# The scan of a Mamba-2 layer taken in pairs of chunks, with one stretch of diagonal matmuls in each pair

## The chip, the cores and the metric

The kernel runs on one core of a Trainium2 chip. The metric is the device time of one execution in microseconds; for the kernel before it is the median of three runs, 1520.32 us (1519.99 to 1521.67). One further execution was profiled; every row of a trace below comes from that one.

## The reference

Two layers on a sequence of 1024 tokens of width 1024, with a residual around each and a norm at the end. The first is a spatial-gating layer (a gated MLP that mixes tokens inside chunks of 128), the second a Mamba-2 mixer. The change touches the second alone. Cut to what matters (G = 8 groups, J = 4 heads a group, P = 64 wide, N = 128 states, chunks of 128 tokens):

```python
proj = h @ w_in                                   # z | x, B, C | dt
xbc = silu(causal_depthwise_conv(xbc, conv_w, conv_b))     # 4 taps along the tokens
dA_cs = cumsum(dt * A, axis=2)                    # inside each chunk
decay = exp(where(causal, seg, -inf))             # seg = dA_cs[l] - dA_cs[s]
cb = einsum('bclgn,bcsgn->bclsg', Cm, Bm)
w_ls = cb * decay * dt
y_diag = einsum('bclsgj,bcsgjp->bclgjp', w_ls, x)          # inside a chunk
states = einsum('bclgn,bclgj,bclgjp->bcgjpn', Bm, decay_to_end * dt, x)
prev = scan(carry * chunk_decay + states)         # state before each chunk
y_off = einsum('bclgn,bcgjpn,bclgj->bclgjp', Cm, prev, exp(dA_cs))
y = y_diag + y_off + x * d_skip
gated = rmsnorm(y * silu(z))  per group;  out = gated @ w_out
```

## The kernel before, in words

Large products run in a split form: each float32 operand is written as a high and a low part, and a product is three matmuls (`mm3`, lines 134 to 136). They are also arranged by Strassen-like schemes of seven block products. The Mamba layer first computes some of its projections into DRAM (z, and x, B, C of groups 0, 1, 3 and 5), then runs the scan, `scans()` (lines 1845 to 1962), and then the rest of the output product, `into_end()`.

The scan goes over 64 steps n, group by group, eight chunks c to a group. Small float32 matmuls of a chunk stand between pieces of a large product that fills TensorE: first the projections that are still missing (x, B, C of groups 2, 4, 6, 7, and z of group 7: the generator `projections()`, lines 1392 to 1455), then the first block product of the output (`bo.product(1)`). `project(upto)` runs that filler up to a count of *units*, one unit being six matmuls of 128x512 in the projections and twice three in the output's product; `want(n)` says how many units have run by step n. A projection of 128 channels is eight units and ends in one of two PSUM buffers, `ab`.

The work of a chunk, by method of the class `Scan`:

- `load`: SP loads the decay sums of the chunk, spread over the partitions, into `wl`.
- `decay`: ACT makes the decay matrix of four heads in place, four Relu of 128x128 and an Exp of 128x512 (lines 1594 and 1596).
- `pe_a`: three transposes and the product of B and C into the PSUM tile `tp` (lines 1588 and 1589).
- `tokens`: DVE scales x by dt and masks the product of B and C (lines 1602 and 1604); ACT copies B (line 1606); POOL scales x again for the state (line 1607).
- `weights`: DVE multiplies decay and masked product, 128x512 (line 1612).
- `pe_b`: the *diagonal*, four matmuls with 64 columns each (line 1621), the *off* product of the last state with C (line 1625), and the chunk's *own* contribution to the state (line 1632). Every third and seventh chunk also sums squares for the group's norm with a column of ones (`sum_b`, line 1697). A float32 matmul shows as two passes in the trace.
- `carry` and `update`: POOL decays the state (line 1642), DVE adds the chunk's own part (line 1651, or a copy at line 1649 for chunk 0).
- `out`: DVE scales the off product (line 1663) and adds the skip to the diagonal (line 1666, twice); POOL adds the two (line 1669).
- `gate`: POOL multiplies by silu(z) (line 1673).

The order is written out by hand, each engine runs its instructions in the order of the program, and waits come from the tiles' reads and writes. In PSUM a whole buffer is guarded: a reader on one engine waits for the earlier users of the same buffer on another. Each buffer kind has a fixed count: `sm` (yy, sp, tp) four, `ab` two, `wl` four.

The convolution of a finished projection is a queue of small steps: one on ACT (line 1323), three taps on DVE (line 1317), and per pair of projections one SiLU on ACT (line 1428). `drain()` takes one entry from the queue; `push` joins the first step of a new projection to the queue's last entry, so that a SiLU and the next projection's first step come out together. At the start of a projection everything older than the last one's own steps is drained at once (line 1440), after the next weights have been prepared (line 1453: a cast on ACT, line 111, and a subtraction on POOL, line 112).

Towards the end the operands of the output's product are prepared between the chunks: `bo.ready` scales them by the norm (DVE, line 1750, twice), `bo.prep` splits them (two casts on ACT, two subtractions on DVE, lines 111 and 112). `gate_half` (line 1679) multiplies half of group 7 by silu(z).

Of the kernel before, what the change touches and what calls it, by code (L numbers as in the profile page):

```python
# [11 lines left out]
ALU = mybir.AluOpType  # L12
# [3 lines left out]
P = 128  # L16
# [6 lines left out]
G = 8  # L23
# [6 lines left out]
def kernel(  # L30
# [1528 lines left out]
    class Scan:  # L1559


        def __init__(self, g, eng):
            self.g, self.st, self.eng = g, sts[g], eng
            self.wl, self.tp, self.cw, self.ps, self.state = {}, {}, {}, {}, {}
            if g < G - 1:
                gd.append(dr.tile([P, 2, T], F32, name=f"g_d{g}"))
            else:
                gd.append(self.st["x"])
# [46 lines left out]
        def pe_b(self, c, ends=None):  # L1615

            w, wl = self.cw[c], self.wl.pop(c)
            yy = sm("yy")
            for j in range(4):
                pt, f = j // 2, j % 2  # L1620
                nc.tensor.matmul(out=yy[f * 64:(f + 1) * 64, pt * P:(pt + 1) * P], lhsT=w[:, j * 64:(j + 1) * 64],  # L1621
                                 rhs=wl[:, j, :], start=True, stop=True)
            if c > 0:
                for pt in range(2):
                    nc.tensor.matmul(out=yy[:, 256 + pt * P:384 + pt * P],  # L1625
                                     lhsT=self.state[c - 1][:, pt * P:(pt + 1) * P], rhs=self.x(3, c),
                                     start=True, stop=True)
            sp = None
            if c < 7 or ends is not None:
                sp = sm("sp")  # L1630
            if c < 7:
                nc.tensor.matmul(out=sp[:, 0:256], lhsT=w[:, 512:640], rhs=w[:, 256:512], start=True, stop=True)  # L1632
            if ends is not None:
                ends.sum_b(sp[:, 256:512], 2 if ends.g == G - 1 else 1)
            self.ps[c] = yy, sp
# [10 lines left out]
        def update(self, c):  # L1646
            if c == 0:
                self.state[0] = k1([P, 256], "state")
                V.tensor_copy(out=self.state[0], in_=self.ps[0][1][:, 0:256])
            elif c < 7:  # L1650
                V.tensor_tensor(out=self.state[c], in0=self.ps[c][1][:, 0:256], in1=self.state[c], op=ALU.add)
# [7 lines left out]
        def out(self, c):  # L1659
            yy, t2 = self.ps.pop(c)[0], self.y(c)  # L1660
            if c > 0:
                t1 = k1([P, 2, P], "t1")
                V.tensor_tensor(out=t1, in0=yy[:, 256:512].rearrange("p (m l) -> p m l", m=2),
                                in1=self.st["ze", c // 4][:, 2:4, c % 4 * P:c % 4 * P + P], op=ALU.mult)
            for pt in range(2):
                V.scalar_tensor_tensor(t2[:, pt, :], self.x(pt, c), dsk[:, 2 * self.g + pt:2 * self.g + pt + 1],
                                       yy[:, pt * P:(pt + 1) * P], ALU.mult, ALU.add)
            if c > 0:
                self.eng.tensor_tensor(out=t2, in0=t2, in1=t1, op=ALU.add)
# [23 lines left out]
        def sum_b(self, pr=None, n=1):  # L1693
            pr = sm("pr") if pr is None else pr
            for m in range(n):
                for h in range(2):
                    nc.tensor.matmul(out=pr[h * 64:h * 64 + 1, 0:256], lhsT=ones[:, 0:1],
                                     rhs=self.sq[:, m, h * 256:(h + 1) * 256], start=m == 0, stop=m == n - 1)
            self.sr = self.sq[:, 1, 0:256]
            for h in range(2):  # L1700
                nc.scalar.copy(out=self.sr[h * 64:h * 64 + 1], in_=pr[h * 64:h * 64 + 1, 0:256])
# [143 lines left out]
    def scans():  # L1845
# [41 lines left out]
        drain(len(queue))  # L1887
        project(AHEAD)
        at("pe_a", 1), at("tokens", 1), at("weights", 1)
        at("load", 2)  # L1890
        for n, (g, c) in enumerate(chunks):
            if n == M + 3:
                drain(len(queue))
            elif n == N - 9:
                for k in range(2):
                    bo.get("a", 0, 0, k)
            elif n == N - 7:
                end["scan"] = scan[G - 1]
                bo.get("b", 0, 0, 0)
            p = g if c >= 4 else g - 1  # L1900
            at("pe_b", n, scan[p] if c % 4 == 3 and p >= 0 else None)
            project(want(n + .5))
            at("pe_a", n + 2)
            if n > 0:
                at("weights", n + 1)
            at("update", n)
            at("out", n)
            at("decay", n + 2)
            at("carry", n + 1)
            drain()  # L1910
            at("tokens", n + 2)
            at("gate", n)
            if n >= N - 7:
                k = n - N + 7
                if k % 2:
                    bo.prep(1, k // 2)
                else:
                    bo.ready(0, 0, k // 2)
            at("load", n + 3)
            th = 0 if c >= 4 else 1  # L1920
            if p >= 0:
                sc = scan[p]
                if p == G - 1:
                    if c == 5:
# [6 lines left out]
            if c % 4 == 0 and n >= 8:  # L1931
                scan[g - 1].sum_c(1 - th)
# [19 lines left out]
        bo.prep(1, 3)  # L1952
# [63 lines left out]
```

## Time and profile before

| | |
|---|---|
| median of three runs | 1520.32 us (1519.99 to 1521.67) |
| the profiled execution | 1518.62 us, its span 1516.8 us |
| clock of TensorE in it | 0.995 of full |
| the scan's 64 chunks | 1020.6 to 1359.4 us of the span |
| busy in the span | PE 97%, DVE 69%, ACT 52%, POOL 27% |

Starts are counted from the span's first instruction. PE is TensorE, DVE is VectorE, ACT is ScalarE, POOL is GpSimd, SP issues the DMAs. A row of the timeline shows the start, the length up to the end of the last of its instructions, the engine, the line, the operation, what it writes and reads, its form and how many instructions it joins; in brackets stands the idle time before it and what ended it. Matmuls are pipelined, so their lengths overlap, and the distance from start to start is what one costs. For a matmul 128*64 means 128 rows and 64 columns of the array.

### The profile page before, as it was taken

What the parts mean: (1) busy time and instruction counts of PE and PEld (TensorE: products, weight loads), DVE (VectorE), ACT (ScalarE), POOL (GpSimd) and SP (SyncE); (2) the same over time, 40 slices, a digit from 0 to 9 for tenths busy, and PEclk for the clock granted to TensorE, in tenths of its full rate; (3) what the DMA queues carried; (4) which work ended last, traced back from release to release, by engine and by line L of the source; (5) the groups of instructions that cost most, each with busy time, mean ns of one, the idle gap of its engine ahead of it and who ended that gap; (6) DMA issues with size and microseconds to landing.
All of it is one profiled execution on the core that took longest, in us unless ns stands there. A gap on an engine that the chain in (4) does not pass through costs nothing. (4 is left out here: it accounts for less than half of the span.)

```text
span 1516.8 us, 21309 instructions
## 1 busy us (share of the span) xinstructions
PE 1475.7 (97%) x7834; PEld 1219.7 (80%) x7834; DVE 1051.7 (69%) x1713; ACT 782.8 (52%) x1257; POOL 402.5 (27%) x451
## 2 busy tenths in 40 slices
PE   6899999999999999999999999999999999999997
PEld 6899988888888888877778888877777777777875
DVE  6966567676666655678656467867677776688876
ACT  6533332232323445556565556666676666756463
POOL 1111010000000023202131222217677666643121
PEclk9999999999999999999999999999999999999999
DMA  5554323323322999947277978677656564579973
GB/s 183 140 167 139 111 90 103 116 103 103 116 77 86 356 251 244 258 139 160 98 179 155 201 153 167 144 245 202 188 162 173 160 189 137 168 252 278 258 151 111
DMA packets 174952, 254.45 MB, mean 168 GB/s; under 512 B 16400, under 2 KB 103168, under 8 KB 171648
## 3 DMA queue, kind: packets, MB, share of 16 engines
q1 hardware_dynamic: 124768, 168.93, 36.1%
q0 software_dynamic: 42448, 70.27, 23.1%
q10 hardware_dynamic: 7632, 13.90, 2.5%
q8 instruction: 62, 1.02, 0.3%
q14 instruction: 42, 0.34, 0.1%
HBM read 186.14 MB, written 51.18 MB: 156 GB/s over the span
## 5 line engine op out<-in xcount | busy, mean ns | idle before, releaser
L134 PE MATMUL acc<-hh,wh 128*128 128x512 f32 x868 | 340.3, 392 | 2.5 <-ACT u L296 2.0
L136 PE MATMUL acc<-hh,wl 128*128 128x512 f32 x868 | 338.6, 390 | 2.0 <-DVE wl L112 1.8
L135 PE MATMUL acc<-hl,wh 128*128 128x512 f32 x868 | 337.9, 389 | 0.0
L112 DVE TENSOR_TENSOR wl<-wr,wh 128x1024 fp32r<-128x1024 f32 (+1 forms) x96 | 114.3, 1192 | 119.0 <-ACT wh L111 118.8
L136 PEld LDWEIGHTS acc<-hh,wl 128*128 128x128 f32 x868 | 162.9, 188 | 37.9 <-DVE wl L112 3.7
L134 PEld LDWEIGHTS acc<-hh,wh 128*128 128x128 f32 x868 | 163.0, 188 | 37.3 <-ACT u L296 3.6
L135 PEld LDWEIGHTS acc<-hl,wh 128*128 128x128 f32 x868 | 163.1, 188 | 33.2
L296 ACT COPY u<-acc 128x512 f32<-128x512 f32 x115 | 66.7, 582 | 198.5 <-PE acc L136 198.3
L111 ACT CAST wh<-wr 128x1024 fp32r<-128x1024 f32 (+1 forms) x112 | 115.2, 1029 | 95.7 <-PE acc L135 56.7
L136 PE MATMUL acc<-wh,hl 128*128 128x256 f32 x448 | 129.3, 289 | 4.0 <-DVE hl L407 3.5
L134 PE MATMUL acc<-wh,hh 128*128 128x256 f32 x448 | 129.6, 289 | 3.2 <-DVE wh L418 1.6
L135 PE MATMUL acc<-wl,hh 128*128 128x256 f32 x448 | 128.7, 287 | 1.3 <-DVE wl L421 1.3
L134 PE MATMUL ab<-hh,wh 128*128 128x512 f32 x288 | 128.2, 445 | 1.5 <-DVE x L1317 1.1
L136 PE MATMUL ab<-hh,wl 128*128 128x512 f32 x288 | 113.4, 394 | 0.0
L135 PE MATMUL ab<-hl,wh 128*128 128x512 f32 x288 | 112.4, 390 | 0.0
L136 PEld LDWEIGHTS acc<-wh,hl 128*128 128x128 f32 x448 | 87.8, 196 | 5.2 <-DVE hl L407 4.2
L134 PEld LDWEIGHTS acc<-wh,hh 128*128 128x128 f32 x448 | 87.8, 196 | 4.2 <-ACT hh L400 1.9
L135 PEld LDWEIGHTS acc<-wl,hh 128*128 128x128 f32 x448 | 87.8, 196 | 1.7 <-DVE wl L421 1.5
L1594 ACT ACTIVATE wl<-wl,tk 128x128 f32<-128x128 f32 x256 | 81.6, 391 | 1.5 <-DMA wl<-cs_d 1.3
L649 POOL DMA_DIRECT2D y_d<-y x8 | 4.4, 548 | 290.7 <-DVE y L646 290.7
L135 PE MATMUL bo<-wl,xh 128*128 128x512 f32 x192 | 75.9, 395 | 3.9 <-DVE wl L742 2.1
L112 DVE TENSOR_TENSOR wl<-t,wh 128x1024 fp32r<-128x1024 f32 (+1 forms) x38 | 45.4, 1196 | 47.7 <-ACT wh L111 47.6
(316 smaller groups left out, 3251.1 us busy)
## 6 DMA issues: line engine op xcount, KB each, us to landing
wr<-in_a_w_in_dram SPq DMA_DIRECT2D x48, 512.0 KB, 3.7
wl<-cs_d SPq DMA_DIRECT2D x64, 256.0 KB, 3.3
wr<-in_b_w_in_dram SPq DMA_DIRECT2D x30, 512.0 KB, 7.7
wb<-in_a_w_out_dram SPq DMA_DIRECT2D x10, 1024.0 KB, 10.9
wb<-in_b_w_out_dram SPq DMA_DIRECT2D x10, 1024.0 KB, 11.1
wr<-in_b_w_in_dram SPq DMA_DIRECT2D x36, 256.0 KB, 7.1
v<-v_d SPq DMA_DIRECT2D x8, 1024.0 KB, 4.9
y_d<-y POOLq DMA_DIRECT2D x8, 1024.0 KB, 5.7
```

The source lines that it names most:

```text
L111: nc.scalar.copy(out=hi, in_=src)
L112: return (eng or nc.vector).tensor_tensor(out=lo, in0=src, in1=hi.bitcast(F32), op=ALU.subtract)
L134: nc.tensor.matmul(out=o, lhsT=l[0], rhs=r[0], start=start, stop=False, **kw)
L135: nc.tensor.matmul(out=o, lhsT=l[0], rhs=r[1], start=False, stop=False, **kw)
L136: nc.tensor.matmul(out=o, lhsT=l[1], rhs=r[0], start=False, stop=stop, **kw)
L296: nc.scalar.copy(out=self.u[n][:, i], in_=a)
L649: store = lambda: nc.gpsimd.dma_start(out=y_d[-1], in_=y)
L1594: nc.scalar.activation(wl[:, j, :], wl[:, j, :], AF.Relu, scale=-1.0, bias=tokc(2, c, self.g)[:, j:j + 1])
```

## The change

The chunks are taken in pairs, the even one n and the odd one n+1:

- `pe_b` becomes three methods. `diagonal(n)` does the diagonals of both chunks, into one `yy` buffer; `own` and `off` write one buffer `os` and are called for each chunk on its own. In the even step comes the diagonal, then own and off of n; in the odd step own and off of n+1, followed at once by `pe_a`.
- `out` becomes `skip` (the skip and the diagonal, for both chunks in the even step) and `out` (the off product and the sum).
- `sum_b` goes behind the diagonal, a chunk later than before, with 64 columns of ones in place of one, into a buffer of its own; `sum_c`, which stores its result, follows in the same step.
- The convolution's `drain` comes first on DVE in the even step, and after `out` and `gate` in the odd one.
- `decay` runs three chunks ahead instead of two, and ahead of the filler and of `out`; `weights` two ahead instead of one; `load` goes out in pairs, four and five ahead.
- Carrying and updating the state come ahead of `out`.
- The output's operands (`ready`, `prep`) and `gate_half` of group 7's first half come a chunk sooner, the fourth `prep` inside the loop.
- Before the loop, `pe_a`, `tokens` and `weights` of chunk 1 come ahead of the filler.

```diff
-        def pe_b(self, c, ends=None):
+        def diagonal(self, c):
...
+            yy = sm("yy")
+            for e in range(2):
+                w, wl = self.cw[c + e], self.wl.pop(c + e)
+                self.yy[c + e] = yy[:, e * 256:(e + 1) * 256]
+                for j in range(4):
+                    pt, f = j // 2, j % 2
+                    nc.tensor.matmul(out=self.yy[c + e][f * 64:(f + 1) * 64, pt * P:(pt + 1) * P],
+                                     lhsT=w[:, j * 64:(j + 1) * 64], rhs=wl[:, j, :], start=True, stop=True)
+        def own(self, c):
+            w = self.cw[c]
+            if c < 7:
+                self.os[c] = sm("os")
+                nc.tensor.matmul(out=self.os[c][:, 0:256], lhsT=w[:, 512:640], rhs=w[:, 256:512],
+                                 start=True, stop=True)
+        def off(self, c):
+            if c == 7:
+                self.os[c] = sm("os")
             if c > 0:
                 for pt in range(2):
-                    nc.tensor.matmul(out=yy[:, 256 + pt * P:384 + pt * P],
+                    nc.tensor.matmul(out=self.os[c][:, 256 + pt * P:384 + pt * P],
...
+        def skip(self, c):
+            yy, t2 = self.yy.pop(c), self.y(c)
             for pt in range(2):
                 V.scalar_tensor_tensor(t2[:, pt, :], self.x(pt, c), dsk[:, 2 * self.g + pt:2 * self.g + pt + 1],
                                        yy[:, pt * P:(pt + 1) * P], ALU.mult, ALU.add)
+        def out(self, c):
+            os, t2 = self.os.pop(c), self.y(c)
             if c > 0:
+                t1 = k1([P, 2, P], "t1")
+                V.tensor_tensor(out=t1, in0=os[:, 256:512].rearrange("p (m l) -> p m l", m=2),
+                                in1=self.st["ze", c // 4][:, 2:4, c % 4 * P:c % 4 * P + P], op=ALU.mult)
                 self.eng.tensor_tensor(out=t2, in0=t2, in1=t1, op=ALU.add)
...
-                    nc.tensor.matmul(out=pr[h * 64:h * 64 + 1, 0:256], lhsT=ones[:, 0:1],
+                    nc.tensor.matmul(out=pr[h * 64:h * 64 + 64, 0:256], lhsT=ones[:, 0:64],
...
+        at("pe_a", 1), at("tokens", 1), at("weights", 1)
         project(AHEAD)
-        at("pe_a", 1), at("tokens", 1), at("weights", 1)
-        at("load", 2)
+        at("load", 2), at("load", 3)
+        at("decay", 2)
         for n, (g, c) in enumerate(chunks):
...
-            at("pe_b", n, scan[p] if c % 4 == 3 and p >= 0 else None)
-            project(want(n + .5))
-            at("pe_a", n + 2)
-            if n > 0:
-                at("weights", n + 1)
-            at("update", n)
+            if c % 2 == 0:
+                at("diagonal", n)
+                if c % 4 == 0 and g > 0:
+                    scan[g - 1].sum_b()
+                elif n == N - 2:
+                    scan[g].sum_b(n=2)
+                at("own", n), at("off", n)
+                at("load", n + 4), at("load", n + 5)
+                drain()
+                at("skip", n), at("update", n)
+                at("carry", n + 1)
+                at("skip", n + 1)
+                project(want(n + .5))
+                at("pe_a", n + 2)
+                if c % 4 == 0 and g > 0:
+                    scan[g - 1].sum_c(1 if c else 0)
+            else:
+                at("own", n), at("off", n)
+                at("pe_a", n + 2)
+                at("update", n)
+                at("carry", n + 1)
+            at("tokens", n + 2)
+            at("weights", n + 2)
+            at("decay", n + 3)
+            if c % 2:
+                project(want(n + .5))
             at("out", n)
-            at("decay", n + 2)
-            at("carry", n + 1)
-            drain()
-            at("tokens", n + 2)
             at("gate", n)
-            if n >= N - 7:
-                k = n - N + 7
+            if c % 2:
+                drain()
+            if n >= N - 8:
+                k = n - N + 8
                 if k % 2:
                     bo.prep(1, k // 2)
                 else:
                     bo.ready(0, 0, k // 2)
-            at("load", n + 3)
...
-                    if c == 5:
+                    if c == 4:
                         sc.gate_half(th), sc.squares(th)
...
-            if c % 4 == 0 and n >= 8:
-                scan[g - 1].sum_c(1 - th)
...
-        bo.prep(1, 3)
         sc.gate_half(1), sc.squares(1)
```

More of the change, by code (lines that the diff above doesn't have):

```diff
@@ L1563, in __init__ @@
             self.g, self.st, self.eng = g, sts[g], eng
-            self.wl, self.tp, self.cw, self.ps, self.state = {}, {}, {}, {}, {}
+            self.wl, self.tp, self.cw, self.yy, self.os, self.state = {}, {}, {}, {}, {}, {}
             if g < G - 1:
@@ L1613, in weights @@
                             op=ALU.mult)
-        def pe_b(self, c, ends=None):
-            w, wl = self.cw[c], self.wl.pop(c)
+        def diagonal(self, c):
             yy = sm("yy")
[L1619 to L1622, printed above, removed]
+            for e in range(2):
[14 more added lines that the diff above has]
+                self.os[c] = sm("os")
             if c > 0:
                 for pt in range(2):
-                    nc.tensor.matmul(out=yy[:, 256 + pt * P:384 + pt * P],
+                    nc.tensor.matmul(out=self.os[c][:, 256 + pt * P:384 + pt * P],
                                      lhsT=self.state[c - 1][:, pt * P:(pt + 1) * P], rhs=self.x(3, c),
                                      start=True, stop=True)
[L1628 to L1635, printed above, removed]
         def carry(self, c):
@@ L1648, in update @@
                 self.state[0] = k1([P, 256], "state")
-                V.tensor_copy(out=self.state[0], in_=self.ps[0][1][:, 0:256])
+                V.tensor_copy(out=self.state[0], in_=self.os[0][:, 0:256])
             elif c < 7:
-                V.tensor_tensor(out=self.state[c], in0=self.ps[c][1][:, 0:256], in1=self.state[c], op=ALU.add)
+                V.tensor_tensor(out=self.state[c], in0=self.os[c][:, 0:256], in1=self.state[c], op=ALU.add)
         def y(self, c):
@@ L1657, in y @@
             return self.cw[c][:, 768:1024].rearrange("p (m l) -> p m l", m=2)
[L1659 to L1664, printed above, removed]
+        def skip(self, c):
+            yy, t2 = self.yy.pop(c), self.y(c)
             for pt in range(2):
@@ L1896, in scans @@
                     bo.get("a", 0, 0, k)
+            elif n == N - 8:
+                bo.get("b", 0, 0, 0)
             elif n == N - 7:
                 end["scan"] = scan[G - 1]
-                bo.get("b", 0, 0, 0)
             p = g if c >= 4 else g - 1
-            at("pe_b", n, scan[p] if c % 4 == 3 and p >= 0 else None)
-            project(want(n + .5))
-            at("pe_a", n + 2)
-            if n > 0:
-                at("weights", n + 1)
-            at("update", n)
+            if c % 2 == 0:
[24 more added lines that the diff above has]
+                project(want(n + .5))
             at("out", n)
-            at("decay", n + 2)
-            at("carry", n + 1)
-            drain()
-            at("tokens", n + 2)
             at("gate", n)
-            if n >= N - 7:
-                k = n - N + 7
+            if c % 2:
+                drain()
+            if n >= N - 8:
+                k = n - N + 8
                 if k % 2:
```

## The prediction, made before the changed kernel was run

> **What bounds the kernel now.** I read first the page's span, then the windows of the scan, then the waits of TensorE inside it, then the timelines.
>
> ```profile
> span 1516.8 us, 21309 instructions
> ```
>
> ```profile
> 1020.60:1309.60 289.00, 286.81 (x1745) 219.11 (x1744) 210.00 (x437) 195.03 (x406) 200.52 (x222) 1.00 0.61 170
> 1309.60:1359.40 49.80, 48.87 (x301) 36.13 (x301) 38.33 (x81) 35.53 (x71) 23.43 (x29) 1.00 0.76 254
> ```
>
> The columns of the windows are the stretch, its length, and the busy time of PE, weight loads, DVE, ACT and POOL. The first is chunks 0 to 53 of the scan, the second chunks 54 to 63. TensorE is busy throughout at full clock, DVE 210.00 of 289.00 us in the first and 38.33 of 49.80 us in the second. TensorE sets the time; it hardly waits:
>
> ```profile
> PE ab L134 <- DVE x L1317: 1.1, 2, 0.7
> PE bo L135 <- DVE wl L112: 0.7, 1, 0.7
> PE sp L1697 <- POOL gsq L1691: 0.5, 1, 0.5
> ```
>
> That is 2.3 us in 338.8. So an edit gains what it takes off TensorE's own stream, as long as the other engines still deliver ahead of it.
>
> **What the change takes off TensorE.** One chunk (number 25), by start times:
>
> ```profile
> 1154.19 0.39 PE L136 MATMUL ab<-hh,wl 128*128 128x512 f32 x1
> 1154.51 0.66 PE L1621 MATMUL yy<-wl,cw 128*64 128x128 f32 x8
> 1155.09 0.71 PE L1625 MATMUL yy<-xbc,state 128*128 128x128 f32 x4
> 1155.64 0.60 PE L1632 MATMUL sp<-cw 128*128 128x256 f32 x2
> 1155.89 0.58 PE L134 MATMUL ab<-hh,wh 128*128 128x512 f32 x1
> 1156.31 0.39 PE L135 MATMUL ab<-hl,wh 128*128 128x512 f32 x1
> 1156.54 0.40 PE L136 MATMUL ab<-hh,wl 128*128 128x512 f32 x1
> ...
> 1157.46 0.49 PE L1588 MATMUL tp<-ident,xbc 128*128 128x128 f32 x3
> 1157.79 0.39 PE L1589 MATMUL tp<-xbc 128*128 128x128 f32 x2
> ```
>
> A projection matmul takes 0.23 us (1156.31 to 1156.54), so a unit of six takes 1.4; a 128-column pass takes 0.11 (three from 1157.46 to 1157.79), so pe_a takes 0.55. Around the diagonal, the only 128*64 work, time is lost three times: 0.32 into it instead of 0.23; its eight passes, two column halves at once, take 0.58 instead of 4 x 0.11; the four passes after it 0.55 instead of 0.44. That is 0.09 + 0.14 + 0.11 = 0.34 us a stretch. With 32 stretches instead of 64 the gain is 32 x 0.34 = 10.9 us. Into and out of pe_a nothing is lost, so stretches of other float32 work may move freely.
>
> [...]
>
> ```profile
> 1165.61 0.60 PE L1632 MATMUL sp<-cw 128*128 128x256 f32 x2
> 1166.13 0.60 PE L1697 MATMUL sp<-gsq,ones 128*1 128x256 f32 x4
> 1166.66 0.50 PE L134 MATMUL ab<-hh,wh 128*128 128x512 f32 x1
> 1167.00 0.39 PE L135 MATMUL ab<-hl,wh 128*128 128x512 f32 x1
> ```
>
> The norm's sum (128*1, another mode) makes L1632 to L135 1.39 us instead of 0.67 (1155.64 to 1156.31): 0.72. Behind the diagonal with 64 columns it is in the diagonal's mode: two pairs of 256-column passes at (0.67 - 0.23) / 2 = 0.22, so 0.44; if they didn't pair, 0.88 (a loss of 0.16 each). The 128*1 passes start in pairs, four in 0.53, so I take 0.44: 15 sums in the scan x 0.28 = 4.2 us. If all 2.3 us of waits goes too, the gain is 10.9 + 4.2 + 2.3 = 17.4 us.
>
> **What the new order makes late.** A pair on TensorE, from the first diagonal: eight diagonal pitches 0.9; exit and first load 0.2, own 0.44, off 0.44: 2.0; a unit, 3.4; pe_a(n+2), 3.95; a unit, 5.35; own and off of the odd chunk, 6.2; pe_a(n+3), 6.8; two units, 9.6. DVE's steps are these:
>
> ```profile
> 1166.43 0.41 DVE L1602 TENSOR_TENSOR cw<-tp,tk 128x256 f32<-128x256 f32 x1
> 1166.76 0.27 DVE L1604 TENSOR_TENSOR cw<-tp,mask 128x128 f32<-128x128 f32 x1
> 1167.12 0.95 DVE L1612 TENSOR_TENSOR wl<-wl,cw 128x512 f32<-128x512 f32 x1
> 1168.10 0.42 DVE L1651 TENSOR_TENSOR state<-sp,state 128x256 f32<-128x256 f32 x1
> 1168.45 0.41 DVE L1663 TENSOR_TENSOR t<-yy,ze 128x256 f32<-128x256 f32 x1
> 1168.78 0.60 DVE L1666 SCALAR_TENSOR_TENSOR cw<-xbc,dsk,yy 128x128 f32<-128x128 f32 x2
> 1169.29 1.27 DVE L1317 SCALAR_TENSOR_TENSOR x<-ab,par,x 128x1021 f32<-128x1021 f32 x1
> ```
>
> In the odd chunk tokens start at 7.1 and take 0.7, weights end at 8.75, the off product's scaling (L1663) at 9.1 and the tap, now last, at 10.3. The next diagonal, at 9.7, needs only the weights: an ordinary pair holds, with 0.9 us to spare. The first tap, the skips and the update of the even chunk end near 3.3, ahead of pe_a(n+2). So the 32 pairs cost nothing in themselves; four places do.
>
> *The buffer of ab.* A product's first unit writes the buffer that the third tap of the product two before it read. A product (128 channels) is 8 units; by chunk c 16 + 112c/50 of them have run, rounded down, half a chunk counting too. Its steps join the queue after its eighth unit, and each drain takes one. Counted so from the code, units 33, 65 and 105, each the first of a product, are the second unit of the odd chunks 7, 21 and 39, and the third tap that they wait for is the drain of the same chunk. TensorE is there at 6.8 + 1.4 = 8.2; the tap ends at 10.3. Before, a tap stood ahead of tokens, and no such wait shows at these chunks. Three times 2.0 is 6.0 us (with the tap early, 0).
>
> *A tap that waits for ACT.* Where a group's SiLU is forced out by a new product, ACT does this:
>
> ```profile
> 1080.72 1.05 ACT L111 CAST wh<-wr 128x1024 fp32r<-128x1024 f32 x1
> 1081.79 1.28 ACT L1428 ACT_TABLE_LOAD   x1
> 1083.08 1.91 ACT L1428 ACTIVATE bc<-bc 128x2048 f32<-128x2048 f32 x1
> 1085.02 1.21 ACT L1323 ACTIVATE x<-ab,par 128x1024 f32<-128x1024 f32 x1
> 1086.13 1.27 ACT L1594 ACTIVATE wl<-wl,tk 128x128 f32<-128x128 f32 x4
> 1087.41 1.28 ACT L1596 ACT_TABLE_LOAD   x1
> 1088.70 0.63 ACT L1596 ACTIVATE wl<-wl 128x512 f32<-128x512 f32 x1
> ```
>
> ```profile
> 1086.26 1.28 DVE L1317 SCALAR_TENSOR_TENSOR x<-ab,par,x 128x1023 f32<-128x1023 f32 x1 [4.21 <-ACT x L1323]
> ```
>
> This is chunk 11: the tap waits 4.21 us, and none of the waits above is for the weights behind it. After the change the forced part stands behind decay(14), which ends at 9.9 (tokens, a copy, 1.9 of decay): cast, table, SiLU and convolution's first step end at 15.2, or 5.6 in the next pair. Queued behind that tap on DVE are a second tap, the skips and update(12), done at 8.9; off(13) wants that state at 7.6: 1.3 us. Tokens(14) follow at 9.4, and ACT's decay(15) behind them, with its table load 3.2 us, ends at 13.4, the weights at 14.4; TensorE is there at 12.8: 1.6. Chunk 11 costs 2.9. At chunk 25 the next pair has a unit less ahead of off, which is there at 5.8 against 8.9, and 1.6 again: 4.7. Chunk 46, worked likewise, 2.4. At 4, 18 and 32 the part falls ahead of a decay with room. Bounds: 0, as now, and 10.0; I take 9, nearest the end that the written order gives.
>
> *The last chunks.* Here DVE has little room, since the output's operands join it:
>
> ```profile
> 1346.13 1.23 DVE L112 TENSOR_TENSOR xl<-ya,xh 128x1024 fp32r<-128x1024 f32 x1 [1.74 <-ACT xh L111]
> ...
> 1350.72 1.92 DVE L1750 SCALAR_TENSOR_TENSOR ya<-ya,par,rb 128x512 f32<-128x512 f32 x2
> ```
>
> A chunk sooner they end the odd chunk, so their casts stand on ACT behind decay(n+3) instead of ahead of the next one's, and their splits (1.23 each) ahead of the next pair's skips. After chunk 57 DVE splits from 2.9 to 5.2 in pair 58; then skips, update, tokens, weights, scaling, the scale of 1.9, update, tokens and weights again end at 11.6, where TensorE, with three units, is ready at 8.5. In pair 60, behind z's SiLU, the splits begin at 4.7; off waits 1.8, and with gate_half (1024 columns, so about a split's 1.23) the weights are 2.8 late. Together 7.7. The lower bound is the 0.7 of wait that this part has now; I take 7. Earlier operands (prep at 59 instead of 60) remove that 0.7, already in the 2.3.
>
> *The rest.* Two taps flushed ahead of chunk 53's update: 0 to 2, taken 1. The loads go out on SP two at a time, behind the wait for the diagonal, 1.0 us into the pair; behind them queue sum_c, the stores and the prefetches, which nobody awaits inside the pair.
>
> ```profile
> wl<-cs_d SPq DMA_DIRECT2D x64, 256.0 KB, 3.3
> ```
>
> They land near 5, and the first decay that reads them stands behind tokens(n+3), at 8: nothing lost, and 1 us a pair if landing took twice as long. In the prologue pe_a(1) only moves ahead of seven units.
>
> **Sum.** 6 + 9 + 7 + 1 = 23 against 17.4: 5.6 us longer. The profiled execution took 1518.62 us (span 1516.8); the median of the runs shown, 1520.32, lies 1.7 above it. 1518.6 + 5.6 + 1.7 = 1525.9; with the roundings, all upward by a tenth or two, 1525.
>
> **Rivals.** *The stream alone decides* (faster): at chunks 11, 25, 46 and in the last ten DVE, 73% busy in the first window, catches up within the pair, and only the waits for ab stand: 1520.3 - 17.4 + 6 = 1508.9, or 1502.9 without them. The point is whether the even chunk's update ends before the odd chunk's off product, about 6 us into the pair. For it speak TensorE's 286.81 of 289.00 us, and that chunk 11 costs nothing that the waits show now; against it, that taps and splits queue in order ahead of update and weights. Chance 0.17. *Half*: waiting taps cost nothing, the rest stands: 1525 - 9 = 1516; with half the tail too, 1512.5. Chance 0.2. *More contention* (slower still): the product of weights spreads from 678 to 1983 ns.
>
> ```profile
> L1612 DVE TENSOR_TENSOR wl<-wl,cw x63: 678/951/1983, 1021.8 to 1353.7; 128x512 f32<-128x512 f32 x63
> ```
>
> At the longest it ends 1.0 us later than worked above, 0.1 past the 0.9 to spare; with POOL behind too, 0.3 us in 25 pairs gives 1533. Chance 0.1. *The modes don't pair*: sums at 0.88 and no gain from them: 6.6 us more, 1532; 0.03. The forecast keeps 0.5, with its own range from 1519 to 1533.
>
> **How the numbers follow.** A measurement tells about 0.2% from no change, here 3 us: 1517.3 to 1523.3. Faster: 0.17, and two thirds of the 0.2, makes 0.3. Same: the rest of it and the lower end of the forecast, 0.21. Slower: 0.49. The range 1508 to 1533 leaves out a tenth at either end.
>
> **What would show it.** Right: TensorE's shortest chunk pair shorter by 0.3, diagonals of 16 in a row; waits of ab's matmul for a tap near 2 us, three times; of the off product for the state; of the diagonal for weights; waits in the scan of 15 us or more. Wrong: waits under 8 us there, or the last ten chunks shorter than 48 us; then the time is under 1517.

## The result, and the profile after

The changed kernel is slower: 1533.39 us in the median of four runs (1530.39 to 1534.85), against 1520.28 us before (1519.99 to 1521.67, four runs). The ratio is 1.0087, with a 95% interval of 1.0075 to 1.0099: 13.1 us longer. I had forecast 1525 with a range from 1508 to 1533, so the direction came out and the size did not: about 5 us were forecast and 13 measured.

The profiled execution after took 1533.07 us. Its span, and the windows that answer the two shown of before (columns: the stretch, its length, busy PE, weight loads, DVE, ACT, POOL, then the granted clock):

```profile
span 1531.4 us, 21280 instructions
```

```profile
1020.60:1316.60 296.00, 279.42 (x1745) 226.06 (x1744) 213.07 (x432) 192.61 (x407) 196.72 (x220) 0.99 0.59 166
1316.60:1373.00 56.40, 48.71 (x303) 38.40 (x303) 42.62 (x88) 37.92 (x72) 27.03 (x31) 0.97 0.71 225
```

The span is 14.6 us longer. Chunks 0 to 53 take 296.0 us in place of 289.0, the last ten 56.4 in place of 49.8, and 1.0 us is lost behind the scan. TensorE's busy time in the first stretch fell from 286.81 to 279.42 us: the gain is there. But TensorE now stands still for 16.6 us of that stretch instead of 2.2, and the clock is no longer 1.00 in either. The waits of TensorE (what waits and for whom; us in total, times, the longest):

```profile
PE yy L1623 <- DVE wl L1612: 9.6, 8, 2.5
PE os L1640 <- DVE state L1658: 6.0, 4, 3.0
PE ab L134 <- DVE bc L1317: 5.4, 3, 2.1
...
PE os L1631 <- issue: 2.4, 2, 1.6
...
PE ab L134 <- DVE x L1317: 0.9, 1, 0.9
```

These are 24.3 us, where the same view of before has 2.9 in all (its three largest rows are the prediction's 2.3). The diagonal (line 1623) waits for the weights, the off product (line 1640) for the state, a projection's first matmul for the tap that still reads its buffer. The stream itself looks as forecast; this is where a pair begins, chunk 16, on TensorE:

```profile
1105.36 1.22 PE L1623 MATMUL yy<-wl,cw 128*64 128x128 f32 x16
1106.40 0.60 PE L1706 MATMUL pr<-gsq,ones 128*64 128x256 f32 x4
```

Sixteen diagonal passes stand in a row, 1.04 us from first to the next line, where two stretches of eight took 0.58 each, with two entries and two exits around them. A pair of chunks with four units and no wait takes 9.60 us from diagonal to diagonal, in place of 9.97.

And these are the places where TensorE stands still in the scan (the bracket is its idle time and what ended it):

```profile
1060.25 0.50 PE L134 MATMUL ab<-hh,wh 128*128 128x512 f32 x1 [1.64 <-DVE bc L1317]
...
1091.37 0.49 PE L1640 MATMUL os<-xbc,state 128*128 128x128 f32 x2 [1.25 <-DVE state L1658]
...
1096.61 0.44 PE L1623 MATMUL yy<-wl,cw 128*64 128x128 f32 x4 [0.60 <-DVE wl L1612]
...
1119.55 0.50 PE L134 MATMUL ab<-hh,wh 128*128 128x512 f32 x1 [0.93 <-DVE x L1317]
...
1139.11 0.50 PE L134 MATMUL ab<-hh,wh 128*128 128x512 f32 x1 [1.71 <-DVE bc L1317]
...
1169.81 0.58 PE L1640 MATMUL os<-xbc,state 128*128 128x128 f32 x1 [3.03 <-DVE state L1658]
...
1213.61 0.38 PE L1640 MATMUL os<-bc,state 128*128 128x128 f32 x1 [0.73 <-DVE state L1658]
...
1219.86 0.33 PE L1623 MATMUL yy<-wl,cw 128*64 128x128 f32 x2 [1.59 <-DVE wl L1612]
...
1240.74 0.50 PE L134 MATMUL ab<-hh,wh 128*128 128x512 f32 x1 [2.05 <-DVE bc L1317]
...
1292.04 0.45 PE L1631 MATMUL os<-cw 128*128 128x256 f32 x1 [1.58 <-issue]
...
1296.63 0.44 PE L1623 MATMUL yy<-wl,cw 128*64 128x128 f32 x4 [0.73 <-DVE wl L1612]
...
1306.99 0.44 PE L1623 MATMUL yy<-wl,cw 128*64 128x128 f32 x4 [0.54 <-DVE wl L1612]
...
1318.18 0.44 PE L1623 MATMUL yy<-wl,cw 128*64 128x128 f32 x4 [0.95 <-DVE wl L1612]
...
1348.16 0.66 PE L1623 MATMUL yy<-wl,cw 128*64 128x128 f32 x8 [2.53 <-DVE wl L1612]
...
1354.44 0.67 PE L1631 MATMUL os<-cw 128*128 128x256 f32 x2 [0.79 <-issue]
...
1356.06 0.71 PE L1640 MATMUL os<-bc,state 128*128 128x128 f32 x4 [0.95 <-DVE state L1658]
...
1363.13 0.43 PE L1623 MATMUL yy<-wl,cw 128*64 128x128 f32 x3 [2.46 <-DVE wl L1612]
```

The rows at 1060.25, 1139.11 and 1240.74 are the buffer of `ab`, in chunks 7, 21 and 39. Those at 1091.37 and 1096.61, at 1169.81, and at 1292.04 are the taps that wait for ACT, after chunks 11, 25 and 46 (at 1292.04 the trace names no releaser; DVE's tap waited 3.57 us for ACT just before). The rows at 1213.61 and 1219.86 are of the same kind, after chunk 32, where I had said there was room. The row at 1119.55, in chunk 18, is a fourth wait for the buffer of `ab`: the product's first unit stands there in the even chunk, and two taps come in a row on DVE ahead of it, the last of chunk 17 and the first of chunk 18. From 1296.63 to 1318.18 three pairs in a row wait for weights. The last four are the tail. The wait at chunk 18, and then the largest of the body (1169.81), on DVE (the bracket is DVE's idle time):

```profile
1116.91 2.58 DVE L1317 SCALAR_TENSOR_TENSOR x<-ab,par,x 128x1022 f32<-128x1022 f32 x2
...
1166.31 2.60 DVE L1317 SCALAR_TENSOR_TENSOR x<-ab,par,x 128x1023 f32<-128x1023 f32 x2 [6.02 <-ACT x L1323]
...
1169.34 0.42 DVE L1658 TENSOR_TENSOR state<-os,state 128x256 f32<-128x256 f32 x1
```

At 1166.31 DVE has stood still for 6.02 us in front of a tap, with the skips and the state's update queued behind it, and the off product starts when the state is there. At the tail's first large wait it is the scale of the output's operands that stands in the way:

```profile
1344.59 1.87 DVE L1759 SCALAR_TENSOR_TENSOR ya<-ya,par,rb 128x512 f32<-128x512 f32 x2
1346.38 0.41 DVE L1658 TENSOR_TENSOR state<-os,state 128x256 f32<-128x256 f32 x1
...
1347.41 0.69 DVE L1612 TENSOR_TENSOR wl<-wl,cw 128x512 f32<-128x512 f32 x1
```

The weights at 1347.41 are what the diagonal at 1348.16 waits for.

One thing was not in my sum at all. Behind three of the waits TensorE runs on at 0.54 to 0.57 of its clock; the fourth window is behind the wait of 2.53 us (the clock is the third number from the end):

```profile
1169.90:1173.50 3.60, 3.60 (x14) 3.33 (x15) 3.10 (x9) 2.61 (x6) 2.33 (x4) 0.57 0.07 25
1240.80:1244.80 4.00, 4.00 (x22) 3.03 (x24) 1.88 (x4) 3.97 (x4) 3.92 (x4) 0.57 0.00 0
1364.20:1367.80 3.60, 3.60 (x15) 2.52 (x12) 3.34 (x7) 0.94 (x3) 1.11 (x1) 0.54 0.81 299
...
1348.20:1351.80 3.60, 3.60 (x27) 2.86 (x28) 0.24 (x1) 3.55 (x7) 1.06 (x2) 1.00 0.49 182
```

In 3.6 us at 0.57 some 1.5 us of work are lost, an estimate (3.6 x 0.43); the three together are 1.5 + 1.7 + 1.7 = 4.9 us.

### The profile page after: what moved, and what is told of

Its sections match the earlier page's. It is cut to its first block, busy times and chain, and to the rows that moved or that the text cites. A ratio compares the mean times of both kernels' runs of the same rounds, so it can differ in the third digit from the quotient of the medians.

```text
span 1531.4 us, 21280 instructions
## 1 busy us (share of the span) xinstructions
PE 1466.5 (96%) x7834; PEld 1227.5 (80%) x7834; DVE 1057.5 (69%) x1713; ACT 781.1 (51%) x1257; POOL 400.9 (26%) x451
## 5 line engine op out<-in xcount | busy, mean ns | idle before, releaser
L134 PE MATMUL ab<-hh,wh 128*128 128x512 f32 x288 | 122.4, 425 | 8.0 <-DVE bc L1317 5.4
```

The lines of the kernel that those rows point to most:

```text
L134: nc.tensor.matmul(out=o, lhsT=l[0], rhs=r[0], start=start, stop=False, **kw)
```

## The experiments

My theory after the result: the gain on TensorE's stream is real, the body's loss comes from where the convolution's steps stand on DVE, the tail's loss from the output's operands coming a chunk sooner, and the halved clock from the waits themselves. The rivals: DVE is short of time however it is ordered; the tail's loss is the pairing; the halved clock has another cause; TensorE's stream does not decide. Times are medians, ratios are against the kernel before, measured beside each. Traces are of one execution each. Pair lengths are the distances between the first diagonal passes of the pairs, and "the tail" is the time from chunk 54's diagonal to the output's eighth unit: 48.6 us before and 55.2 after.

### The sums alone, in the old buffer

In the kernel before, the sum takes 64 columns of ones and goes from the end of `pe_b` to between the diagonal and the off product:

```diff
-                    nc.tensor.matmul(out=pr[h * 64:h * 64 + 1, 0:256], lhsT=ones[:, 0:1],
+                    nc.tensor.matmul(out=pr[h * 64:h * 64 + 64, 0:256], lhsT=ones[:, 0:64],
...
+            if ends is not None:
+                ends.sum_b(sp[:, 256:512], 2 if ends.g == G - 1 else 1)
```

> The kernel before, with one part of the change alone: the sums take 64 columns of ones and stand right behind the diagonal stretch, so no switch of tile shape lies between them. If a switch costs what the rows of before gave (0.28 us for each of 15 sums), the time falls by 4.2 us, from 1520.3 to 1516.1, and the sums' two passes start 0.21 us apart. If TensorE's stream does not decide at these places, the time stays at 1520.3 within 1 us.

1527.33 us, ratio 1.0054 (1.0034 to 1.0073): neither. The pairs with a sum and no new wait are shorter by 0.28 us, 9.97 in place of 10.25, which is the term. But there is a new row among the waits of TensorE:

```profile
PE sp L1634 <- ACT gsq L1701: 7.1, 7, 2.7
```

The chunk's own product writes the other half of the sum's buffer, and now waits until ACT has copied the sum out of it. So the buffer was to be separated.

### The sums alone, in a buffer of their own

The same edit, with `sum_b` called so that it takes a buffer itself:

```diff
-                ends.sum_b(sp[:, 256:512], 2 if ends.g == G - 1 else 1)
+                ends.sum_b(n=2 if ends.g == G - 1 else 1)
```

> The kernel before, with the sums as after the change: 64 columns of ones, right behind the diagonal, and now in a buffer of their own, so that the chunk's own product no longer waits for ScalarE to copy the sum out. If a switch of tile shape costs 0.28 us for each of 15 sums, 1516.1. If the gain is swallowed by another wait, 1520.3 or more.

1517.27 us against 1518.85, ratio 0.9987 (0.9978 to 0.9997). The waits for the copy are gone, and the gain is 1.6 us of 4.2. At one place most of the rest goes: the pair of chunk 50 takes 14.1 us in place of 11.3, with this row in TensorE's timeline:

```profile
1292.89 0.44 PE L1697 MATMUL pr<-gsq,ones 128*64 128x256 f32 x2 [1.84 <-POOL gsq L1691]
```

The sum now stands ahead of the off product, and POOL has not yet added the squares. The clock in the 3.6 us behind this wait was 0.61.

### The same, with chunk 51's sum last again

```diff
+            at51 = ends is not None and (ends.g, c) == (5, 3)
-            if ends is not None:
+            if ends is not None and not at51:
                 ends.sum_b(n=2 if ends.g == G - 1 else 1)
...
+            if at51:
+                ends.sum_b()
```

The second call stands behind the chunk's own product.

> The kernel before, with the sums as after the change in a buffer of their own, but in chunk 51, where the sum behind the diagonal waited 1.8 us for GpSimd's addition and the pair took 14.1 us against 11.3, the sum stands last again. If that one place took the rest of the gain, it falls from 1517.3 by about 2.8 to 1514.5. If the gain of a switch was only 1.6 us in all, it stays at 1517.

1516.48 us against 1519.30, ratio 0.9985 (0.9976 to 0.9994). It is faster than both kernels. The pair of chunk 50 fell from 14.1 to 11.6 us, but the time lies between the two that were expected, and its interval overlaps that of the run above. The medians differ by 2.8 us, the profiled scan (first diagonal to the output's eighth unit) is 334.3 us against 337.6, 3.2 shorter. So two thirds to three quarters of the term of 4.2 are there, and it is the part of the change that pays alone.

### The diagonals apart again

```diff
-            for e in range(2):
-                w, wl = self.cw[c + e], self.wl.pop(c + e)
+            w, wl = self.cw[c], self.wl.pop(c)
...
-                at("own", n), at("off", n)
+                at("diagonal", n), at("own", n), at("off", n)
                 at("pe_a", n + 2)
-                at("update", n)
+                at("skip", n), at("update", n)
```

The last lines are those of the odd step.

> The kernel after, with one part undone: each chunk's diagonal in its own step again, with a buffer of its own, all else in pairs. If the fewer switches gave the 10.9 us that the rows of before say, and a diagonal that comes 6 us later no longer waits for its weights (9.6 us of waits, of which I take 5 to 8 away), the time is 1533.4 + 10.9 less 5 to 8, 1536 to 1539. If the fewer switches gave nothing, because VectorE decides, it is 1525 to 1533.

1544.83 us, ratio 1.0165 (1.0148 to 1.0182): 11.4 us more than with pairs, where I expected 3 to 6. The pairs without a wait are longer by 0.33 to 0.37 us (9.15 to 9.52, 10.97 to 11.30), so the gain of 0.34 a stretch is confirmed. The waits for weights are no longer among the longest, and the tail falls to 51.2. In their place this stands among the waits of TensorE:

```profile
PE tp L1588 <- DMA xbc<-xbc_d: 9.0, 5, 3.1
```

The transposes wait for the prefetched x, B and C. That the odd chunk's skip, a step later here, holds the buffer longer and so delays the prefetch fits, but is only argued.

### The output's operands later again

```diff
-            if n >= N - 8:
-                k = n - N + 8
+            if n >= N - 7:
+                k = n - N + 7
...
-                    if c == 4:
+                    if c == 5:
                         sc.gate_half(th), sc.squares(th)
```

(The load of the first weights and the fourth `prep` also go back to their places of before.)

> The kernel after, with one part undone: the output's operands (scale, casts, splits, the last gate) a chunk later, as in the kernel before. If this part is what lengthens the stretch from chunk 54 to the output's eighth unit from 48.6 to 55.2 us, that stretch falls back by 5 to 6.6 us and the time to 1527 to 1528. If it is the pairing, which asks for the weights of two chunks at once, the stretch stays at 55 and the time at 1533.

1537.02 us, ratio 1.0120 (1.0100 to 1.0140). Neither: the tail rose to 59.6 us instead of falling. The earlier operands are worth 4.4 us to the paired order, and my theory of the tail falls.

### The last ten chunks apart

```diff
-                at("diagonal", n)
+                at("diagonal", n, 2 if n < N - 10 else 1)
...
+                if n >= N - 10:
+                    at("diagonal", n, 1)
```

The last two lines stand first in the odd step.

> The kernel after, with the diagonals of the last ten chunks apart again, each in its own step. If it is the pairing that lengthens the tail, since it asks for the odd chunk's weights 5 us sooner, the stretch from chunk 54 to the output's eighth unit falls from 55.2 to about 51, as with all diagonals apart, and the time to 1529. If VectorE's work in those chunks is too much however it is ordered, the stretch stays above 54 and the time at 1532 to 1535.

1529.87 us, ratio 1.0074 (1.0059 to 1.0089), as expected of the pairing. From chunk 54 on, to the same point, in the window that answers the one of 56.40 us:

```profile
1317.50:1370.00 52.50, 48.62 (x303) 37.18 (x303) 41.13 (x88) 37.81 (x72) 27.01 (x30) 1.00 0.73 242
```

52.5 us in place of 56.4, at full clock, though each pair has its second switch again. (The difference rests on the profiles: the intervals of the two ratios overlap.) In this order the scale ahead of the odd chunk's weights hurts only if the next diagonal wants those weights at once. That the pairing alone lengthens the tail does not follow: the next two runs keep the diagonals of the tail in pairs, and their tails are 50.7 and 51.7 us.

### Both steps in the middle of the pair

```diff
-                drain()
                 at("skip", n), at("update", n)
                 at("carry", n + 1)
                 at("skip", n + 1)
+                drain(), drain()
...
-            if c % 2:
-                drain()
```

> The kernel after, with both convolution steps of a pair behind the even chunk's update and second skip, in place of one first and one last. If the order on VectorE is the cause, the waits of the projection's first matmul for a tap (6.3 us) and of the off product for the state (6.0 us) go, with the slow clock behind two of them (3 us), and a part, some 3 to 5 us, comes back as waits of the diagonal for weights, since the tokens now stand behind a tap that waits for ScalarE: 1521 to 1524. If VectorE is short of time altogether, the waits only change their place: 1531 to 1535.

1542.42 us, ratio 1.0154 (1.0126 to 1.0181): worse than either theory. The waits of TensorE:

```profile
PE yy L1623 <- DVE wl L1612: 12.7, 11, 2.5
...
PE ab L134 <- DVE x L1317: 9.2, 4, 3.6
...
PE ab L134 <- DVE bc L1317: 4.0, 2, 2.3
```

The waits for the state are gone, but those for the taps grew from 6.3 to 13.2 us, and those for weights from 9.6 to 12.7. ACT holds the taps up less than before: up to chunk 54 DVE waits for ACT's first step 9.2 us in all, where it waited 34.2 in the change. Both taps now stand behind the skips and the update, so they end later; at chunk 18, on DVE and then on TensorE:

```profile
1120.89 2.59 DVE L1317 SCALAR_TENSOR_TENSOR x<-ab,par,x 128x1022 f32<-128x1022 f32 x2
```

```profile
1123.53 0.79 PE L134 MATMUL ab<-hh,wh 128*128 128x512 f32 x1 [3.61 <-DVE x L1317]
```

### The steps five microseconds apart

```diff
-            if c % 2:
+            if c % 2 == 0:
                 drain()
```

> The kernel after, with the pair's second convolution step at the end of the even chunk's work instead of the odd one's, so that the steps stand some 5 us apart. If the steps' places are the cause of the body's loss, the waits for a tap's buffer (5.4 us) go, most of those for the state (6.0 us) too, and with them the halved clock behind two of them (3 us): 1520 to 1524. If a step ahead of the odd chunk's update only makes that update and the weights late, the waits for weights grow by as much: 1531 to 1536.

1528.51 us, ratio 1.0065 (1.0047 to 1.0082), between the two. The three waits for `ab` at chunks 7, 21 and 39 are gone but for 0.2 us at chunk 7, and at chunk 54 the kernel is 1.9 us ahead of the change (294.1 against 296.0). But now others come, at chunks 32 and 46 among them. DVE and then TensorE in the timeline at chunk 32:

```profile
1199.48 1.27 DVE L1317 SCALAR_TENSOR_TENSOR x<-ab,par,x 128x1021 f32<-128x1021 f32 x1
```

```profile
1200.81 0.50 PE L134 MATMUL ab<-hh,wh 128*128 128x512 f32 x1 [3.79 <-DVE x L1317]
```

Here the third tap is the step at the end of the even chunk, and the new product begins in that chunk's second half, ahead of it.

The edit reaches the tail too, where the queue still hands out z's SiLU. In the change the last of it comes out at the end of chunk 59, ahead of the casts of the output's operands; here no step is taken there, and it comes out at the start of chunk 60, behind them. ACT in the change, and then here:

```profile
1350.80 1.03 ACT L1418 ACTIVATE z<-ab 128x1024 f32<-128x1024 f32 x1
1351.72 1.04 ACT L111 CAST xh<-ya 128x1024 fp32r<-128x1024 f32 x1
```

```profile
1348.85 1.03 ACT L111 CAST xh<-ya 128x1024 fp32r<-128x1024 f32 x1
...
1352.78 1.02 ACT L1418 ACTIVATE z<-ab 128x1024 f32<-128x1024 f32 x1
```

DVE's split waits 2.03 us for the cast here and 4.36 in the change. The wait of 2.53 us at chunk 60's pair stays, those of 0.79, 0.95 and 2.46 behind it are gone (one of 0.54 comes), and the tail is 51.7 us with its diagonals in pairs. With both steps in the middle of the pair the SiLU is also behind the casts, and the tail 50.7. So the tail's 55.2 takes both, the paired diagonals and the SiLU ahead of the casts.

### Both of these together, and a mixture

With the last ten chunks apart, the one has the edit above, and the other this:

```diff
-            if c % 2:
+            if (c % 2 == 0) == (n - n % 2 in (6, 12, 18, 20, 26, 36, 38, 52)):
                 drain()
```

> The kernel after, with the steps 5 us apart and the last ten chunks' diagonals apart. If the two causes lie in different places and each is as supposed, their gains add: 1533.4 less 9 to 13 less 4, 1516 to 1520, about the kernel before or under it. If either falls, it comes out where the other alone does, 1520 to 1530.

> The kernel after, with the last ten chunks' diagonals apart, and the second convolution step at the end of the even chunk only in the pairs that were shorter with it there (chunks 6, 12, 18, 20, 26, 36, 38 and 52), elsewhere at the end of the odd one. If each step's place is good or bad by the product's phase at that pair alone, the pairs' gains add: 11.8 us off the 1529.9 of the kernel with the tail apart, 1518. If the waits only move to the next pair, 1524 to 1530.

1528.40 us (ratio 1.0064, 1.0049 to 1.0080) and 1527.62 us (1.0058, 1.0044 to 1.0072). The gains do not add. In the first of the two the tail is 50.8 us, 0.9 less than with the spaced steps alone, which had taken back most of the tail's loss already, and chunk 54 begins at 295.9 us, with the same order of steps that gave 294.1. In the mixture the chosen pairs did get shorter (chunk 38's pair from 12.4 to 9.2, chunk 26's from 14.4 to 9.6), but the pairs of chunks 10 and 24, which had no wait in the change and 0.5 us at most with the spaced steps, took 14.3 and 15.9 us in place of 9.6 and 11.0, with new waits for `ab` of 2.69 and 3.04 us. The wait moves with the queue.

### A step in each chunk, as before

With the last ten chunks apart, one step stands in the even and one in the odd step, in place of first and last:

```diff
                 at("skip", n + 1)
+                drain()
...
                 at("carry", n + 1)
+                drain()
             at("tokens", n + 2)
```

> The kernel after, with the last ten chunks' diagonals apart, and one convolution step in each chunk behind the update and ahead of the tokens, where the kernel before has it; so the steps stand a chunk apart, and the diagonals still in pairs. If the steps' places made the body's loss, the waits for a tap's buffer (5.4 us), most for the state (5.0) and the halved clock behind them (3) go from the 1529.9 of the kernel with the tail apart, against some 6 us of weights that end 0.4 us late in the sixteen shorter pairs: about 1522. If weights behind a step are late by more, in every pair, the waits of the diagonal for weights grow past 15 us and the time past 1530.

1536.75 us, ratio 1.0117 (1.0091 to 1.0144). Neither: the diagonal's waits for weights fell to 2.7 us, but the waits of TensorE now have this:

```profile
PE yy L1623 <- ACT cw L1606: 9.0, 2, 4.9
```

The diagonal waits twice for ACT's copy of B, which stands in ACT's queue behind a forced cast, table load, SiLU and first step (1.03, 1.28, 1.92 and 1.18 us, from 1204.96 on, ahead of the diagonal at 1213.29; there the copy waited 1.93 us more for DVE's masking, line 1604). Where the kernel before puts its steps, the paired order has no more room than elsewhere.

### The clock behind a wait

The kernel before, made to wait:

```diff
+            for _ in range({9: 16, 13: 20, 17: 24, 21: 28, 25: 32, 29: 20, 33: 24, 37: 28, 42: 32}.get(n, 0)):
+                s_ = scan[g].state[c]
+                V.tensor_scalar(s_, s_, 1.0, None, ALU.mult)
             at("update", n)
```

> The kernel before, with idle work on VectorE (multiplications of the state by one) ahead of the state's update in chunks 9 to 42: 16, 20, 24, 28, 32, 20, 24, 28 and 32 of them, so that the off product behind waits between 1 and some 6 us. If TensorE's clock is halved by the wait itself, the passes behind the waits of 3 us or more run at 0.21 us in place of 0.11 for some 3 us (1.5 us more each), and those behind waits under 2 us mostly at full speed. If the slow passes of the changed kernel came from something else, all of these stay at full speed.

1578.28 us, one run. The nine waits came out between 1.08 and 10.80 us. Two of them in TensorE's timeline, and then the windows behind them:

```profile
1217.66 0.68 PE L1625 MATMUL yy<-xbc,state 128*128 128x128 f32 x4 [1.84 <-DVE state L1651]
...
1271.37 1.20 PE L1625 MATMUL yy<-bc,state 128*128 128x128 f32 x4 [3.67 <-DVE state L1651]
```

```profile
1217.70:1221.30 3.60, 3.60 (x21) 3.12 (x22) 3.00 (x10) 0.00 (x0) 2.87 (x4) 1.00 0.15 38
1271.40:1275.00 3.60, 3.60 (x11) 3.09 (x12) 3.51 (x9) 0.00 (x0) 2.85 (x4) 0.54 0.27 91
```

The waits of 1.08 and 1.84 us cost themselves and nothing more: their pairs are longer than before by 1.12 and 1.87. The one of 3.67 made its pair 5.3 us longer, 1.6 more than itself; the one of 10.80 made it 13.1 longer, 2.3 more. All seven waits of 2.6 us and more are followed by a slow stretch (behind the one of 2.61 us it begins only after a second wait, of 0.83). So the slow clock came behind waits alone here, without the rest of the change.

Whether it does is not settled by the length of the wait. The runs with the spaced steps have the same wait of 3.79 us at chunk 32, without and with the tail apart; the windows behind it, in this order:

```profile
1200.90:1204.50 3.60, 3.60 (x14) 3.11 (x15) 0.00 (x0) 3.57 (x4) 1.83 (x1) 0.66 0.99 275
```

```profile
1201.40:1205.00 3.60, 3.60 (x21) 3.16 (x22) 1.03 (x3) 3.57 (x4) 1.86 (x1) 1.00 1.03 289
```

The pair of chunk 32 took 16.7 us in the one and 15.0 in the other. Behind their wait of 3.28 us at chunk 46 it is the other way round, 1.00 and 0.50. So the price of such a wait differed between these two executions.

## Why the prediction came out too low

**The gains held.** 0.34 us a stretch is 0.33 to 0.37 between the paired kernel and the one apart; 0.28 us a sum is 0.28, and the sums run in pairs; the waits of before are gone from their places. I had 17.4 us, and nothing in the runs speaks for less, save that the sums alone gave 2.8 of 4.2. The sign that I named, the shortest pair shorter by 0.3, holds for pairs with the same work (9.97 to 9.60), not for the shortest of all, which is 8.14 us before, at chunk 48, and 8.50 after, at chunk 58.

**The costs, term by term**, in the idle time of the rows above, against the forecast:

| term | forecast, us | measured, us |
|---|---|---|
| buffer of `ab`, chunks 7, 21, 39 | 6 | 1.64 + 1.71 + 2.05 = 5.40 |
| the same at chunk 18 | 0 | 0.93 |
| taps waiting for ACT, chunks 11, 25, 46 | 9 | 1.85 + 3.03 + 1.58 = 6.46 |
| the same at chunk 32 | 0 | 0.73 + 1.59 = 2.32 |
| pairs of chunks 50, 52 and 54 | 1 (the flush) | 0.73 + 0.54 + 0.95 = 2.22 |
| last chunks | 7 | 2.53 + 0.79 + 0.95 + 2.46 = 6.73 |
| halved clock behind three waits | 0 | 4.9 (estimate) |
| behind the scan | 0 | 1.0 |
| sum | 23 | 30.0 |

30.0 less 17.4 is 12.6, and the span grew by 14.6. The 2.0 that is missing I did not trace. The two short waits that were put into the kernel before cost 0.04 and 0.03 us beyond their length; at that price some twenty waits would make under 1 us of it, an estimate.

The mechanisms that were forecast came, and the sum was wrong. The three `ab` waits came in the chunks and at the size forecast, the taps' waits in the order described, and the two large waits of the tail at 2.53 and 2.46 us where 3.1 and 2.8 were worked out. Two statements failed. First, "TensorE is busy throughout at full clock": I priced every wait at its own length, and behind three of them the clock was 0.54 to 0.57, an estimated 4.9 us. That is the largest missing term, and in part chance: its size is that of the one execution that was profiled. Second, "So the 32 pairs cost nothing in themselves; four places do", with "At 4, 18 and 32 the part falls ahead of a decay with room": at chunk 32 it had no room (2.3 us), at chunk 18 a fourth wait for `ab` was missed (0.9), and the pairs of chunks 50 to 54 wait for their weights (2.2 where 1 was put). The taps at chunks 11, 25 and 46 were put 2.5 too high instead.

**The tail** was priced right, and of its mechanism a part holds. I wrote that the operands a chunk sooner would be the cost. Putting them later again made the tail 4.4 us longer; taking the pairing out of the last ten chunks made it 3.9 shorter. But I had also written that in pair 60 the splits stand behind z's SiLU, and that holds: with the SiLU behind the casts the paired tail is 3.4 us shorter, and taking the pairing out as well saves only 0.9 more. The scale stands in the way because the paired diagonal wants the odd chunk's weights at the start of the next pair.

**The rivals.** *The stream alone* fell: the off product waited for the state four times, 6.0 us. *Half* fell with it, since taps and tail cost their price. *More contention* had the right time, 1533, in the main from the wrong cause: the product of weights still takes 956 ns in the median (951 before), and pairs without a late step run at 9.60 and 10.97 us with no wait. But the longest product takes 2.61 us (1.98 before), at 1214.69, in the unbroken row of DVE ahead of the wait of 1.59 us at 1219.86; that wait, which the table puts to ACT, fits the rival as well. *The modes don't pair* fell by the sum's 0.28.

**What stays open.** Five orders of the convolution's steps were tried, and none brings the paired body under the 289.0 us of before: 296.0 (the change), 307.1, 294.1, 293.9 and 301.7. The third of these was 295.9 in a second kernel with the same order, so a difference of 2 us between them tells nothing. Whether some order would, and why the one that was best leaves 5 us, the runs do not settle. That DVE is short of time altogether is not shown either: it is busy 213.07 of 296.00 us. What the runs show is that each order meets the forced work on ACT, or the two buffers of `ab`, at some phase of the product. What decides whether the clock falls behind a wait stays open too.

## What to carry to other kernels

Price a wait of the engine that sets the time not at its length alone: look at the clock behind it (here it fell to 0.61 behind one wait of 1.84 us, and stayed at 1.00 behind one of 2.53), and count with a cost that comes in some executions and not in others (here 1.6 to 2.3 us a wait). Work that recurs with a period of its own (here eight units a product against a pair of chunks) has to be followed through all phases; "there is room" at some of them needs the same working as the places that are late. And a change of many parts is worth taking apart: here one small part, the sums in the diagonal's tile shape and a buffer of their own, is faster alone by 0.15%, while the large gain of the pairing is given back in waits.

## What the runs showed of the hardware

In the changed kernel the granted clock was 0.57 in the 3.6 us behind a wait of 3.03 us (1169.81), 0.57 in the 4.0 us behind one of 2.05 us (1240.74), and 0.54 in the 3.6 us from 1364.20, behind one of 2.46 us (1363.13); behind one of 2.53 us (1348.16) it was 1.00. The slow stretch was short: behind the wait of 3.03 us the projection's matmuls start 0.42 us apart at 1172.33 and 0.22 apart at 1173.09, 3.28 us after the wait's end. Behind the waits of 1.08 and 1.84 us that were put into the kernel before, the clock stayed at 1.00, and behind all of those from 2.6 to 10.8 us it fell, to 0.50 to 0.74 in the windows, at a price of 1.6 to 2.3 us each (the one of 2.61 us, with a second wait behind it, left out). But behind a wait of 1.84 us in another run (the sum at 1292.89) it was 0.61, and behind the same wait of 3.79 us it was 0.66 in one run and 1.00 in another.

A reader of one half of a PSUM buffer also held up a matmul into its other half: the own product waited 7.1 us in all for ACT's copy of the sum, and no longer did once the sum had a buffer of its own. A second reader waited too: in the kernel before, DVE's update at 1080.79 waited 2.31 us for ACT's copy out of the other half. This is how the program's waits are set; whether the memory itself would need it, no run here shows.
